# A trunk of S5, FoX and GLA layers on one core: f6 ahead of s40 in the MLPs, the first S5 layer's start in another order, and the final norm's means ahead of its turns

## The chip, the core and the metric

The program runs on one core of one Trainium2 chip. The metric is the time of one execution in microseconds (us), the median over runs. The engines are PE (matrix products; PEld are its weight loads), DVE (vector), ACT (scalar functions and copies), POOL (general) and SP, which here only issues DMAs. Each engine works through its own queue in order. DMA queue q1 holds the transfers that SP and ACT issue, q0 those that POOL issues.

## The reference

The input is one sequence of 256 positions with 1024 features, in f32. Four layers follow; each adds a mixer, an MLP and a per-layer embedding (PLE) to the residual h. The mixers are S5, FoX, GLA and S5 again.

```
for l in range(4):
    h += mixer_l(rmsnorm(h))                       # s5, fox, gla, s5
    h += relu(rmsnorm(h) @ w1)**2 @ w2             # MLP, 1024 -> 4096 -> 1024
    h += (p[l] @ W_pp) * sigmoid(rmsnorm(h) @ W_pg)
out = rmsnorm(h)

def s5_mixer(xn, ...):                             # 64 groups, 64 complex states each
    u = xn @ w_in
    dt = exp(log_dt); mag = exp(lr * dt)
    ab = mag * (cos(li * dt) + 1j * sin(li * dt))  # the decay of each state
    bbar = (ab - 1) / lambda * b                   # what B becomes
    x = u times bbar, per group
    s = scan over positions: s[t] = ab * s[t-1] + x[t]
    y = real(s times c) + d_skip * u
    z1, z2 = split(gelu(y) @ w_glu)
    return (z1 * sigmoid(z2)) @ w_out
```

rmsnorm divides by the root of the mean square of the 1024 features, so it needs the sum of squares over all of them before anything can be scaled; the kernel multiplies the unscaled products by that root afterwards.

## The kernel before

The residual h stays in the chip's memory with features on the partitions: eight tiles `H[k]` of 128 features by 256 positions, in pairs `HH[k]`. The program is written in a tile framework: the code names tiles and the framework puts the instructions in an order of its own for each engine, by its model of when operands are ready, and gives each tile a buffer. Three things hold that order: `in_order(...)` keeps the named engines in the order of the code, `keep_in_program_order` pins one DMA, and `issue_after(x)` puts what stands under it behind instruction x.

**Weights.** A weight unit is 256 rows by 512 columns. SP loads it as `raw`; ACT makes `whi`, the value rounded to a shorter format (L182), and DVE makes `wlo`, the rest (L184). A product takes three matmuls: whi times both halves of x, and wlo times the upper one. There are three `raw` and four `whi` and `wlo` buffers, so casts run a few units ahead.

**The MLP** works in blocks. `f`c computes hidden block c of 512 (four units of w1, four banks of accumulation): ACT copies a bank to `relu` (L247), DVE adds the other part (L248), squares the positive part (L386), and it is split into `s`. `s`c`r` multiplies block c by two units of w2 into output half r; the sums of four blocks are closed with `y` (also L247, L248). The string `MLP` sets the order of the blocks. Banks come by tag: f0 to f3, f6 and f7 use three banks `wk` and the bank `mk`, f4 and f5 use three `acc` and `mk`. The second products of the first output half use three `acc` and `po`, those of the second half, blocks 0 to 3, three `wk` and `po`, and s41 to s71 two `wk`. So f6, f7 and s01 to s31 share the `wk` banks, and s40 to s70 use others. Each step after the first also calls `further()`, which adds one step of the preparation of the last S5 layer, between the units.

**The first S5 layer's start** is in `s5_start`, branch `if first`. All 32 column pieces of `w_in` are products w0 to w7 of f32 weights without a split (eighths of 512 rows by 256 columns, `raw`, `wh`, `wl` and so on in turn are only their buffers). Step by step:

- PE warms up with 14 products of ones; ACT scales x from h and squares it (`sq`); PE adds the squares up over the features (`mean`, L1287).
- `s5_scalars` makes on DVE the decay's powers (`powers`, `cpow`, `F1`, `F8`), the table `ct` and, on POOL's queue, four DMAs that write it out as `tab` (L845), which is read back spread over partitions as `coef`.
- `z(0)`: the root. DVE makes `rrow` (L340), POOL raises it to the power −1/2 (L344). `z(1)`: DVE makes `diag` (L353) from it, and PE spreads that over partitions (L354), giving `rstd`.
- `f(0)`: `s5_spread`, 32 small products on PE (L855) that spread the table for the first quarter, so that the first quarter needs no `coef`.
- `bT` (L868, 512 KB a quarter) and `bc` (L879, 256 KB a quarter) are B and C. The steps named in `FIRST` then run quarter by quarter: `u` (L1165) scales w's product, `i` makes `wh` and `wl` out of bT and the table (L889 to L891), `r` makes `rot` (L911 to L914), `o` makes `qo` from bc (L929 to L933), `x` multiplies u by wh and wl on PE (L999), `y` makes the outputs (L1045).

Before the change bT of the quarters 0 and 1 and bc of quarter 0 are issued ahead of all of this.

**The final norm** (`final`) squares each H[k] on ACT, sums it over the features on PE against a column of 1/1024 (L1339), and turns H[k] to positions on partitions while it multiplies by the gain (L1333). When the last mean is there, DVE, POOL, then DVE and ACT scale the turned tiles by the root and SP writes them out.

Of the kernel before, what the change touches and what calls it, by code (L numbers as in the profile page):

```python
# [12 lines left out]
AF = mybir.ActivationFunctionType  # L13
ALU = mybir.AluOpType
# [20 lines left out]
WARM = 14  # L35


MLP = "f0 f1 f2 s00 f3 s10 s20 s30 s01 s11 f4 s21 f5 s31 s40 f6 f7 s50 s60 s70 s41 s51 s61 s71"


def _turn():
# [22 lines left out]
class Trunk:  # L64
# [783 lines left out]
    def s5_spread(self, b):  # L848

        out = []  # L850
        for i in range(2):
            ps = self.psum()
            for p in range(8):
                for g in range(2):
                    self.nc.tensor.matmul(ps[g * 64:(g + 1) * 64, p * 64:(p + 1) * 64], self.pick[:, p], self.ct[:, i, g, :], start=True, stop=True, skip_group_check=True)  # L855
            out.append(ps)
        return out

# [254 lines left out]
    def s5_start(self, l):  # L1113
# [3 lines left out]
        j = l // 3  # L1117
# [24 lines left out]
            units["h", i] = self.parts(units["h", i])  # L1142

        def w(i, between=None):
            b, i = i // 2, i % 2
            if i == 0:
                us[b] = self.psum((128, 2, T), "acc")
            ps = us[b]
            if first:
                raw = halves[2 * b + i]  # L1150
            else:
                hi, lo = units.pop(("h", 2 * b + i))
            for n in range(2):
                c = slice(n * 128, (n + 1) * 128)
                for k in range(4):
                    if first:
                        nc.tensor.matmul(ps[:, n], raw[:, k, c], x[4 * i + k], start=i == k == n == 0, stop=i == 1 and k == 3, skip_group_check=True)
                    else:
                        self.col(ps[:, n], v["x"][2 * i + k // 2][:, k % 2], hi[:, k, c], lo[:, k, c], i == k == n == 0, i == 1 and k == 3)
                if n == 0 and between:  # L1160
                    between()
# [30 lines left out]
        def j_(b):  # L1192
            bcs[b] = self.s5_fetch_out(j, b, self.tc.keep_in_program_order)
# [73 lines left out]
        if first:  # L1267
            halves = [self.raw0] + [self.half(w_in, i) for i in range(1, 8)]
            x = [self.t4("x", (128, 4, T), tag="x4") for _ in range(2)]
            x = [x[k // 4][:, k % 4] for k in range(8)]  # L1270
            bTs = {0: self.s5_fetch_in(j, 0)}
            j_(0)
            bTs[1] = self.s5_fetch_in(j, 1, self.tc.keep_in_program_order)
            scalars, v["ms"] = self.s5_scalars(j), self.psum((128, 2))

            def scaled(k):

                for i in range(2 * k, 2 * k + 2):
                    nc.scalar.activation(x[i], self.H[i], AF.Identity, scale=self.gains[:, l, i:i + 1])
                sq = self.f2("sq")  # L1280
                nc.scalar.activation(sq, self.HH[k], AF.Square)
                return sq
# [7 lines left out]
            with self.in_order(mybir.EngineType.Activation, mybir.EngineType.PE):  # L1290
# [12 lines left out]
                def between():  # L1303
                    next(scalars)

                    next(scalars)
                    sq.append(scaled(3))

                w(0, between)
# [4 lines left out]
                q.update(drain(scalars))  # L1314
                z(1)
                f(0)
            run("f1 j1")
        return lambda: run(FIRST if first else LATER)

    def final(self, out):  # L1320
# [11 lines left out]
            for half, t in enumerate(halves):  # L1332
                nc.tensor.matmul(hT[k // 4][half][:, k % 4], self.H[k][:, t], gain[:, k], start=True, stop=True)  # L1333

        for k in range(8):
            s = sq[k // 4][:, k % 4]
            nc.scalar.activation(s, self.H[k], AF.Square)
            for half, t in enumerate(halves):
                last = nc.tensor.matmul(ms[:, half:half + 1], s[:, t], self.mean, start=k == half == 0, stop=k == 7, skip_group_check=True)  # L1339
            if k < 6:  # L1340
                turn(k)
        with self.tc.issue_after(last.ins):
            turn(6)
            turn(7)
        r = self.inverse_root(ms)
        for half in range(2):
            o = self.t4("fin", (128, 2, 512))
# [69 lines left out]
```

## Time and profile before

| what | value |
|---|---|
| runs of the kernel | 1466.31, 1454.51, 1462.09 us |
| median | 1462.09 us |
| the profiled execution: its own time | 1458.21 us |
| its span in the profile | 1456.2 us |
| mean granted clock of PE | 0.987 |
| DMA in the span | 254.54 MB, mean 175 GB/s |
| ACT's and POOL's busy time | 717.2 us (49%), 100.9 us (7%) |

The span is the time from the first to the last record of the profiled execution, some 2 us shorter than its time. A row of the timeline gives start and length in us, the engine, the line of the code, the operation, what it writes and reads, how many records are joined in it (an f32 matmul leaves two), and in brackets the idle time of the engine before it with what ended that. A row of the waits gives the total of the waits in us, their number and the longest. A row of the stretches gives from:to, the length, for PE, PEld, DVE, ACT and POOL the busy time and the number of instructions, then PE's granted clock, the DMA share and GB/s. In the chain of work that ended last PE holds 63% of the span and every other engine 2% or less.

### The profile page before, as it was taken

What the parts mean: (1) busy time and instruction counts of PE and PEld (TensorE: products, weight loads), DVE (VectorE), ACT (ScalarE), POOL (GpSimd) and SP (SyncE); (2) the same over time, 40 slices, a digit from 0 to 9 for tenths busy, and PEclk for the clock granted to TensorE, in tenths of its full rate; (3) what the DMA queues carried; (4) which work ended last, traced back from release to release, by engine and by line L of the source; (5) the groups of instructions that cost most, each with busy time, mean ns of one, the idle gap of its engine ahead of it and who ended that gap; (6) DMA issues with size and microseconds to landing.
All of it is one profiled execution on the core that took longest, in us unless ns stands there. A gap on an engine that the chain in (4) does not pass through costs nothing.

```text
span 1456.2 us, 26681 instructions
## 1 busy us (share of the span) xinstructions
PE 1401.7 (96%) x10810; PEld 1264.3 (87%) x10810; DVE 1046.4 (72%) x1651; ACT 717.2 (49%) x1118; POOL 100.9 (7%) x167
## 2 busy tenths in 40 slices
PE   8999999999999999999999999999997899999997
PEld 7799988888998888889989598888996799888897
DVE  8995678775866678887667478786676946766764
ACT  3234564444654655445567355454562345545443
POOL 2000000010010000000004000000003100000020
PEclk9999999999999999999999999999998899999998
DMA  7534555557554456766655356565656545556561
GB/s 255 160 108 121 183 180 188 177 172 222 173 159 133 125 165 189 253 220 186 203 162 161 100 153 197 188 228 166 215 161 202 173 150 179 180 179 201 174 190 58
DMA packets 143227, 254.54 MB, mean 175 GB/s; under 512 B 21648, under 2 KB 32240, under 8 KB 143104
## 3 DMA queue, kind: packets, MB, share of 16 engines
q1 hardware_dynamic: 129856, 227.66, 50.4%
q0 software_dynamic: 7360, 23.73, 4.9%
q10 hardware_dynamic: 5888, 1.44, 0.4%
q8 instruction: 84, 1.38, 0.4%
q14 instruction: 39, 0.32, 0.1%
HBM read 242.15 MB, written 7.86 MB: 172 GB/s over the span
## 4 chain that ended last, share of the span: by engine, by line
PE 63%; DMA 2%; DVE 2%; ACT 2%; issue 0%; DVEq 0%; POOLq 0%; ACTq 0%; SPq 0%
PE wk L237 8%; PE acc L237 7%; PE wk L239 4%; PE wk L201 4%; PE wk L202 4%; PE wk L203 4%; PE acc L201 4%; PE acc L202 3%; PE acc L203 3%; PE acc L239 3%; PE mk L237 3%; PE po L237 2%; PE acc L262 1%; PE acc L261 1%; PE acc L263 1%; PE mk L239 1%
## 5 line engine op out<-in xcount | busy, mean ns | idle before, releaser
L184 DVE TENSOR_TENSOR wlo<-raw,whi 128x1024 fp32r<-128x1024 f32 x404 | 491.6, 1226 | 288.1 <-ACT whi L182 280.7
L182 ACT CAST whi<-raw 128x1024 fp32r<-128x1024 f32 x404 | 420.0, 1049 | 505.2 <-DMA raw<-mlp_w 85.4
L237 PE MATMUL wk<-x,whi 128*128 128x512 f32 x576 | 182.1, 401 | 7.8 <-DVE relu L248 7.8
L239 PEld LDWEIGHTS wk<-x,wlo 128*128 128x128 f32 x576 | 106.9, 191 | 22.9
L237 PE MATMUL acc<-s,whi 128*128 128x512 f32 x384 | 118.4, 397 | 2.7 <-ACT whi L182 2.7
L239 PE MATMUL wk<-x,wlo 128*128 128x256 f32 x576 | 113.3, 281 | 0.0
L237 PEld LDWEIGHTS wk<-x,whi 128*128 128x128 f32 x576 | 92.2, 191 | 11.9 <-DVE relu L248 8.9
L201 PE MATMUL acc<-x,whi 128*128 128x256 f32 x352 | 99.8, 287 | 1.8 <-DVE u L1165 1.0
L203 PE MATMUL acc<-x,wlo 128*128 128x256 f32 x352 | 99.9, 286 | 0.8 <-DVE wlo L184 0.8
L202 PE MATMUL acc<-x,whi 128*128 128x256 f32 x352 | 99.4, 285 | 0.0
L239 PEld LDWEIGHTS acc<-s,wlo 128*128 128x128 f32 x384 | 70.4, 190 | 15.8 <-DVE wlo L184 0.5
L237 PE MATMUL mk<-x,whi 128*128 128x512 f32 x256 | 81.4, 395 | 0.0
L239 PE MATMUL acc<-s,wlo 128*128 128x256 f32 x384 | 74.8, 283 | 0.0
L202 PE MATMUL wk<-s,whi 128*128 128x256 f32 x256 | 72.4, 283 | 0.0
L201 PE MATMUL wk<-s,whi 128*128 128x256 f32 x256 | 72.4, 283 | 0.0
L203 PE MATMUL wk<-s,wlo 128*128 128x256 f32 x256 | 72.3, 283 | 0.0
L201 PEld LDWEIGHTS acc<-x,whi 128*128 128x128 f32 x352 | 66.9, 191 | 3.3 <-issue 1.8
L203 PEld LDWEIGHTS acc<-x,wlo 128*128 128x128 f32 x352 | 67.3, 191 | 1.6 <-DVE wlo L184 1.3
L202 PEld LDWEIGHTS acc<-x,whi 128*128 128x128 f32 x352 | 67.2, 192 | 0.2
L237 PEld LDWEIGHTS acc<-s,whi 128*128 128x128 f32 x384 | 60.0, 189 | 4.5 <-ACT whi L182 2.9
L237 PE MATMUL po<-s,whi 128*128 128x512 f32 x192 | 60.5, 397 | 0.0
L237 PE MATMUL wk<-s,whi 128*128 128x512 f32 x192 | 59.1, 395 | 0.0
(402 smaller groups left out, 3358.3 us busy)
## 6 DMA issues: line engine op xcount, KB each, us to landing
raw<-mlp_w SPq DMA_DIRECT2D x256, 512.0 KB, 4.3
raw<-s_w_glu SPq DMA_DIRECT2D x32, 512.0 KB, 4.2
raw<-ple_gate SPq DMA_DIRECT2D x32, 512.0 KB, 3.5
raw<-fox_w_in SPq DMA_DIRECT2D x24, 512.0 KB, 3.7
raw<-gla_w_in SPq DMA_DIRECT2D x24, 512.0 KB, 3.9
raw<-s_w_out SPq DMA_DIRECT2D x16, 512.0 KB, 4.1
kept<-kept POOLq DMA_DIRECT2D x12, 512.0 KB, 5.2
raw<-s_w_in SPq DMA_DIRECT2D x11, 512.0 KB, 4.9
```

The costliest lines, as they stand in the source:

```text
L182: nc.scalar.copy(hi, raw)
L184: self.last_lo = nc.vector.tensor_tensor(lo, raw, hi.bitcast(F32), ALU.subtract)
L201: mm(ps, hi, x[:, 0], start=first, stop=False, skip_group_check=True)
L202: mm(ps, hi, x[:, 1], start=False, stop=False, skip_group_check=True)
L203: self.last_mm = mm(ps, lo, x[:, 0], start=False, stop=last, skip_group_check=True)
L237: mm(ps[n], hi[:, i, s], v[i], start=first and i == 0, stop=False, skip_group_check=True)
L239: self.last_mm = mm(ps[n][:, 0], lo[:, i, s], v[i][:, 0], start=False, stop=last and i == UK - 1, skip_group_check=True)
L261: mm(ps[half], a[:, 0, t], hi[:, k], start=k0 + k == 0, stop=False)
L262: mm(ps[half], a[:, 0, t], lo[:, k], start=False, stop=False)
L263: mm(ps[half], a[:, 1, t], hi[:, k], start=False, stop=k0 + k == nk - 1)
```

## The change

Three parts. In the MLPs f6 comes ahead of s40 rather than behind it. In the first S5 layer the DMAs of bT 0, bc 0 and bT 1 are issued on POOL's queue behind those that write the table, and the products w2 to w7 are kept behind the last product of `s5_spread`. In the final norm the squares of the first four H are added in pairs on DVE, so that 12 products sum the means rather than 16, and the means stand ahead of the turns of their group.

```diff
-MLP = "f0 f1 f2 s00 f3 s10 s20 s30 s01 s11 f4 s21 f5 s31 s40 f6 f7 s50 s60 s70 s41 s51 s61 s71"
+MLP = "f0 f1 f2 s00 f3 s10 s20 s30 s01 s11 f4 s21 f5 s31 f6 s40 f7 s50 s60 s70 s41 s51 s61 s71"
...
-                    self.nc.tensor.matmul(ps[g * 64:(g + 1) * 64, p * 64:(p + 1) * 64], self.pick[:, p], self.ct[:, i, g, :], start=True, stop=True, skip_group_check=True)
+                    self.last_mm = self.nc.tensor.matmul(ps[g * 64:(g + 1) * 64, p * 64:(p + 1) * 64], self.pick[:, p], self.ct[:, i, g, :], start=True, stop=True, skip_group_check=True)
...
         def w(i, between=None):
+            with self.tc.issue_after(v["mm"].ins) if "mm" in v else nullcontext():
+                product(i, between)
+
+        def product(i, between):
             b, i = i // 2, i % 2
...
-            bTs = {0: self.s5_fetch_in(j, 0)}
-            j_(0)
-            bTs[1] = self.s5_fetch_in(j, 1, self.tc.keep_in_program_order)
             scalars, v["ms"] = self.s5_scalars(j), self.psum((128, 2))
...
                     next(scalars)
+                    bTs[0] = self.s5_fetch_in(j, 0, self.tc.keep_in_program_order)
+                    j_(0)
+                    bTs[1] = self.s5_fetch_in(j, 1, self.tc.keep_in_program_order)
                     sq.append(scaled(3))
...
                 f(0)
+                v["mm"] = self.last_mm
             run("f1 j1")
...
-        for k in range(8):
-            s = sq[k // 4][:, k % 4]
-            nc.scalar.activation(s, self.H[k], AF.Square)
+        def mean(x, first, last):
             for half, t in enumerate(halves):
-                last = nc.tensor.matmul(ms[:, half:half + 1], s[:, t], self.mean, start=k == half == 0, stop=k == 7, skip_group_check=True)
-            if k < 6:
+                self.last_mm = nc.tensor.matmul(ms[:, half:half + 1], x[:, t], self.mean, start=first and half == 0, stop=last, skip_group_check=True)
+
+        for k in range(4):
+            nc.scalar.activation(sq[0][:, k], self.H[k], AF.Square)
+        nc.vector.tensor_tensor(sq[0][:, 0:2], sq[0][:, 0:2], sq[0][:, 2:4], ALU.add)
+        with self.tc.issue_after(self.last_mm.ins):
+            for k in range(2):
+                mean(sq[0][:, k], k == 0, False)
+            for k in range(4):
                 turn(k)
-        with self.tc.issue_after(last.ins):
-            turn(6)
-            turn(7)
+        for k in range(4, 8):
+            nc.scalar.activation(sq[1][:, k - 4], self.H[k], AF.Square)
+        for k in range(4, 8, 2):
+            with self.tc.issue_after(self.last_mm.ins):
+                for i in range(2):
+                    mean(sq[1][:, k + i - 4], False, k + i == 7)
+            with self.tc.issue_after(self.last_mm.ins):
+                for i in range(2):
+                    turn(k + i)
```

On PE in the first layer's MLP, before, where s31 ends (`po_2964`), s40 starts (`acc_3435`, from block 4's `s_3073`); x is the scaled input of the MLP, the numbers tell tiles apart:

```order
L239 MATMUL po_2964<-s_2648,wlo_3390 128x256 x2
L237 MATMUL acc_3435<-s_3073,whi_3441 128x512 x2
L239 MATMUL acc_3435<-s_3073,wlo_3442 128x256 x2
L237 MATMUL acc_3436<-s_3073,whi_3441 128x512 x2
L239 MATMUL acc_3436<-s_3073,wlo_3442 128x256 x2
```

and, still before, where f6 ends and f7 starts:

```order
L237 MATMUL mk_3488<-x_2197,whi_3557 128x512 x2
L239 MATMUL mk_3488<-x_2197,wlo_3558 128x256 x2
L237 MATMUL wk_3613<-x_2194,whi_3619 128x512 x2
L239 MATMUL wk_3613<-x_2194,wlo_3620 128x256 x2
L237 MATMUL wk_3613<-x_2195,whi_3641 128x512 x2
```

On PE after the change f6 follows s31, with three units in `mk` ahead of the first `wk`:

```order
L239 MATMUL po_2964<-s_2648,wlo_3390 128x256 x2
L237 MATMUL mk_3440<-x_2194,whi_3443 128x512 x2
L239 MATMUL mk_3440<-x_2194,wlo_3444 128x256 x2
L237 MATMUL mk_3440<-x_2195,whi_3465 128x512 x2
L239 MATMUL mk_3440<-x_2195,wlo_3466 128x256 x2
L237 MATMUL mk_3440<-x_2196,whi_3487 128x512 x2
L239 MATMUL mk_3440<-x_2196,wlo_3488 128x256 x2
L237 MATMUL wk_3437<-x_2194,whi_3443 128x512 x2
```

and f7 follows s40:

```order
L239 MATMUL acc_3547<-s_3074,wlo_3574 128x256 x2
L237 MATMUL po_3548<-s_3074,whi_3573 128x512 x2
L239 MATMUL po_3548<-s_3074,wlo_3574 128x256 x2
L237 MATMUL wk_3613<-x_2194,whi_3619 128x512 x2
L239 MATMUL wk_3613<-x_2194,wlo_3620 128x256 x2
```

What moved: s40, whose banks nobody near it uses, now stands between the two blocks that share `wk`, and f6 stands right behind s31, which shares `wk` with it too.

On PE at the start of the first S5 layer the pieces of w are those lines with `acc`; `diag,ones` is the root's product, `ct,pick` the spread, `U,wh` the first x. Both orders in one piece, from the first means' end on:

```order
-L1157 MATMUL acc<-x,wl 128x256 x7
-L1287 MATMUL wk<-mean,sq 128x1 x4
-L1157 MATMUL acc<-x,wh 128x256 x8
-L1157 MATMUL acc<-x,wl 128x256
-L1157 MATMUL acc<-x,raw 128x256 x5
+L1288 MATMUL wk<-mean,sq 128x1 x4
+L1161 MATMUL acc<-x,wh 128x256 x8
 L354 MATMUL wk<-diag,ones 128x256
 L855 MATMUL wk<-ct,pick 64x64 x32
```

What moved: half of w2 and w3 stood ahead of the root's product before; now only w1 does, and w2 and w3 (`wl` and `raw`) come behind the spread.

On DVE the same place, before: `F8` and `F` are powers, `rrow` the root's row, `diag` what PE waits for, `dd` and `rot` the steps behind:

```order
L353 TENSOR_SCALAR diag_364<-ident_86,rrow_275 128x128 x2
L706 TENSOR_TENSOR F8_305<-F8_305,prod_215 128x32x2
L704 TENSOR_TENSOR F8_305<-F8_305 128x32x3
L705 TENSOR_TENSOR prod_215<-F8_305 128x96
L704 TENSOR_TENSOR F8_305<-F8_305 128x32x3
L705 TENSOR_TENSOR prod_215<-F8_305 128x96
L706 TENSOR_TENSOR F8_305<-F8_305,prod_215 128x32x3 x2
L825 TENSOR_TENSOR dd_358<-eye16_102,sd_152 32x512
L911 TENSOR_TENSOR rot_442<-F1_304,F8_305 128x1024
```

and after:

```order
L706 TENSOR_TENSOR F8_305<-F8_305,prod_209 128x32x3 x2
L825 TENSOR_TENSOR dd_358<-eye16_102,sd_146 32x512
L911 TENSOR_TENSOR rot_442<-F1_304,F8_305 128x1024
L911 TENSOR_TENSOR scratch_443<-F1_304,F8_305 128x1024
L911 TENSOR_TENSOR rot_700<-F1_304,F8_305 128x1024
L353 TENSOR_SCALAR diag_364<-ident_86,rrow_275 128x128 x2
```

What moved: diag stood ahead of the last powers, dd and the L911 products, and stands behind three of them now.

## The prediction

> **What bounds the kernel now.** I read the page's first lines, then PE's waits, then the timeline around each wait that the change touches, and the granted clock by stretches.
>
> ```profile
> span 1456.2 us, 26681 instructions
> PE 1401.7 (96%) x10810; PEld 1264.3 (87%) x10810; DVE 1046.4 (72%) x1651; ACT 717.2 (49%) x1118; POOL 100.9 (7%) x167
> PE wk L237 <- DVE relu L248: 7.8, 6, 2.5
> ```
>
> PE is busy for 1401.7 of 1456.2 us, so the change, which leaves PE's work nearly as it was, can win at most some of the 54.5 us in which PE stands still, and what PE loses at a lower clock. The third line is the largest entry among PE's waits. Four of its six waits are the places where f7 follows f6, one in each layer's MLP:
>
> ```profile
> 311.86 0.73 PE L237 MATMUL wk<-x,whi 128*128 128x512 f32 x2 [1.17 <-DVE relu L248]
> 652.62 0.73 PE L237 MATMUL wk<-x,whi 128*128 128x512 f32 x2 [2.49 <-DVE relu L248]
> 1000.56 0.74 PE L237 MATMUL wk<-x,whi 128*128 128x512 f32 x2 [1.89 <-DVE relu L248]
> 1365.20 0.74 PE L237 MATMUL wk<-x,whi 128*128 128x512 f32 x2 [1.04 <-DVE relu L248]
> ```
>
> f7 writes the three `wk` banks that f6 has just filled and that ACT and DVE must empty first: 1.17 + 2.49 + 1.89 + 1.04 = 6.59 us. Two of these gaps cost more than their length. In the stretches the column after the five engines is the granted clock:
>
> ```profile
> 653.23:656.64 3.41, 3.41 (x13) 2.93 (x12) 3.33 (x6) 1.24 (x2) 0.00 (x0) 0.50 0.64 174
> 1001.38:1004.80 3.42, 3.42 (x13) 2.85 (x12) 3.05 (x5) 0.95 (x2) 0.00 (x0) 0.50 0.66 196
> 335.79:339.20 3.41, 3.41 (x12) 2.72 (x11) 3.22 (x4) 1.58 (x2) 0.00 (x0) 0.50 0.45 144
> 653.57 1.05 PE L237 MATMUL wk<-x,whi 128*128 128x512 f32 x2
> 654.85 1.05 PE L237 MATMUL wk<-x,whi 128*128 128x512 f32 x2
> 633.17 0.63 PE L237 MATMUL acc<-s,whi 128*128 128x512 f32 x2
> 633.87 0.85 PE L237 MATMUL acc<-s,whi 128*128 128x512 f32 x3
> ```
>
> After the gaps of 2.49 and 1.89 us PE worked one stretch of 3.41 us at clock 0.50. There a group of four (two 512-wide, two 256-wide) takes 654.85 − 653.57 = 1.28 us; at full clock 633.87 − 633.17 = 0.70. One stretch therefore costs 3.41 × (1 − 0.70/1.28) = 1.55 us. The stretches start whole multiples of 3.413 us apart (1001.38 − 653.23 = 102 × 3.413), so the same gap can halve the clock or not, as it falls on that grid. The gaps of 1.17 and 1.04 us halved nothing.
>
> **MLP: f6 before s40.** No instruction is added or removed. With s40 between f6 and f7, f7's `wk` banks have eight groups of 0.70 = 5.6 us in which to be emptied; the worst gap needed 2.5 us. So 6.59 us of waits and 2 × 1.55 = 3.1 us of half clock go. What is late next is the new seam, where f6 now follows s31 and writes banks from which y is still being read. The order starts f6 with its first three or four units in the `mk` bank, 2.1 to 2.6 us of work ahead of `wk`. The seam of the second MLP is the tightest:
>
> ```profile
> 634.09 1.21 DVE L184 TENSOR_TENSOR wlo<-raw,whi 128x1024 fp32r<-128x1024 f32 x1
> 635.23 1.07 DVE L248 TENSOR_TENSOR y<-wk,y 128x256 f32<-128x256 f32 x3
> ```
>
> s31 ends at 633.17. The first of three y additions ends about 635.64, 2.5 us later: just covered. The third unit's wlo is ready at 635.30, 2.1 us after the seam, and the new order wants it after two groups and a half, 1.86 us: 0.3 us of wait. The other layers are earlier or ask less; I take 0.4 us for all four. Bounds: nothing new (gain 9.7), or one gap like the old ones at each seam (a gain of 3.1 to 5). MLP: 6.6 + 3.1 − 0.4 = **9.3 us**. PE's single 2.70 us wait in s70 of the first MLP and its half-clock stretch (the row at 335.79 above) aren't touched, but their place on the grid moves, so 1.6 us may come or go.
>
> **First S5 layer.**
>
> ```profile
> 0.00:11.87 11.87, 7.13 (x44) 6.77 (x45) 9.59 (x67) 7.25 (x15) 4.37 (x21) 0.99 0.78 254
> bT<-s_bT POOLq DMA_DIRECT2D x2, 512.0 KB, 6.8
> bc<-s_bc POOLq DMA_DIRECT2D x1, 256.0 KB, 7.1
> 11.87 3.49 PE L1157 MATMUL acc<-x,raw 128*128 128x256 f32 x8 [2.85 <-DMA raw<-s_w_in]
> 15.77 1.89 PE L1157 MATMUL acc<-x,raw 128*128 128x256 f32 x8
> 17.50 0.95 PE L1287 MATMUL wk<-mean,sq 128*128 128x1 f32 x8
> 16.64 2.13 POOL L845 DMA_DIRECT2D tab<-ct  x4 [11.62 <-ACT ct L840]
> ```
>
> Up to 11.87 us the DMA moved 11.87 × 254 = 3.0 MB, and 1.28 MB of that is the two bT and the bc that the change moves behind the table. At that rate w_in's first half comes several us sooner, so I take the whole 2.85 us wait as gone (bounds 0 and 2.85) and w0 at 9.0. w0's first eight pieces also took 15.29 − 11.87 = 3.42 us where the next eight took 17.50 − 15.77 = 1.73 (15.29 is where the first run ends), half clock again: 1.7 us. Together 4.55 us.
>
> What it adds is a wait. w2 and later products now stand behind the spread, the spread behind the diagonal product, and that waits for DVE:
>
> ```profile
> 12.93 1.48 DVE L929 TENSOR_TENSOR qo<-bc,cpow 128x1280 f32<-128x1280 f32 x1
> 22.81 0.16 DVE L340 TENSOR_SCALAR rrow<-wk 128x2 f32<-128x2 f32 x1 [4.88 <-PE wk L1287]
> 23.97 0.47 DVE L353 TENSOR_SCALAR diag<-ident,rrow 128x128 f32<-128x128 f32 x2
> 25.54 0.67 DVE L825 TENSOR_TENSOR dd<-eye,sd 32x512 f32<-32x512 f32 x1
> 26.14 1.21 DVE L911 TENSOR_TENSOR rot<-F,F 128x1024 f32<-128x1024 f32 x1
> 29.55 0.67 DVE L913 TENSOR_TENSOR rot<-rot,scratch 128x512 f32<-128x512 f32 x1
> 28.76 0.59 PE L354 MATMUL wk<-diag,ones 128*128 128x256 f32 x2
> 31.30 1.56 PE L1157 MATMUL acc<-x,raw 128*128 128x256 f32 x6
> 32.70 3.62 PE L1157 MATMUL acc<-x,wh 128*128 128x256 f32 x16
> ```
>
> In the new order DVE makes diag after the powers of F, dd and three L911 products. dd began at 25.54; without the idle 4.88, the L929 at 12.93 (1.40 to the next start) and diag itself (0.39), which now come elsewhere, that is 18.87; dd takes 26.14 − 25.54 = 0.60 and the three L911 29.55 − 26.14 = 3.41. So diag begins at 22.9 and PE gets it at 23.1. The root isn't what is late: the last means now stand ahead of w1 and end by 15, and POOL's power, behind three more DMA issues (four took 2.13 us, so 1.6), is there by about 16. PE has from 9.0 on w0 and w1 (32 pieces, 4 × 1.73 = 6.9), two means (at most 0.95 each) and the table's 0.5 us between 15.29 and 15.77: free at about 18.4. It then stands for 4.7 us, more than any gap so far, and about 1.0 us is lost at half clock after it (0 to 1.7 by the grid). Diag product and spread take 31.30 − 28.76 = 2.5, w2 and w3 another 32 pieces, 6.9: 23.1 + 2.5 + 1.0 + 6.9 = 33.5 us, against 32.70 before. x0 now stands right behind w3 and needs wl, which DVE ends at about 34.6: from 23.3 it has L913 and L914 (0.6 each), three L929 (1.40 each), and u, two wh and two pairs of small ones, by their starts before 0.9, 2.3, 1.5 and 1.2, 11.3 us in all. With the way to PE, 34.7: PE is 34.7 − 32.7 = 2.0 us later there. bT and bc, issued at 12 to 16 and first read at 24.5, have some 9 us against the 6.8 and 7.1 us that they took.
>
> Against that DVE, which worked on after 22.81 with the idle 4.88 us behind it, is now ahead by about that much, and these waits of PE on it or on what it feeds should go:
>
> ```profile
> 54.93 0.33 PE L999 MATMUL wk<-U,wh 64*64 64x64 f32 x4 [0.52 <-DMA U<-u]
> 58.88 2.08 PE L1045 MATMUL mk<-qo,P 64*64 64x64 f32 x64 [1.64 <-DVE P L1024]
> 70.51 0.39 PE L202 MATMUL acc<-g,whi 128*128 128x256 f32 x1 [0.46 <-DVE g L1229]
> 74.33 0.39 PE L201 MATMUL acc<-g,whi 128*128 128x256 f32 x1 [2.25 <-DVE u L1165]
> ```
>
> 0.52 + 1.64 + 0.46 + 2.25 = 4.9 us in all. Net 4.9 − 2.0 = **2.9 us**; bounds −2.0 (none of these waits goes) and 4.9 (the later start at x0 is made up).
>
> **The final norm.**
>
> ```profile
> 1445.08 0.95 PE L1339 MATMUL wk<-mean,sq 128*128 128x1 f32 x8
> 1445.89 0.47 PE L1333 MATMUL mk<-gain,h 128*128 128x128 f32 x2
> 1447.19 0.16 DVE L340 TENSOR_SCALAR rrow<-wk 128x2 f32<-128x2 f32 x1 [3.25 <-PE wk L1339]
> 1439.60 0.76 DVE L471 TENSOR_TENSOR z<-wk,rstd 128x256 f32<-128x256 f32 x2 [4.80 <-PE wk L203]
> ```
>
> Four of 16 mean products go; eight records, 1445.89 − 1445.08 = 0.81 us of PE's path. The DVE addition that replaces them lies where DVE has time (its idle 4.80 us); PE runs without a gap there, and the last means still come last but for four turns, so the root and the end move by as much: **0.8 us**. It is at least 0 (if the last turns bind instead) and hardly more, since nothing else of the chain is touched.
>
> **Sum.** 9.3 + 2.9 + 0.8 = 13.0 us. The profiled execution took 1458.2, which makes 1445.2. It lies 3.9 below the median of the runs, 1462.09; the mean of these four executions is 1460.3. I go from there: **1447 us**, 1.0% below the median.
>
> **Rivals.** (1) The S5 layer gives nothing or loses: DVE's stall of 4.7 us is sure by the order, while the later waits go only if DVE keeps its lead. Its bound of −2.0 makes 1452. (2) The seam takes over part of the MLP's wait: the y additions and the casts share DVE, and one old-size gap in two layers, 2 × 2.5, makes 1452. (3) The other side: every f6 starves at its seam. Four units' casts, at 1.21 us of DVE each, are asked for in 2.6 us. From 1.9 us, with the half clock 3.45 per layer, four seams eat the 13.4 us that the rest brings; at 2.5 each they cost 4 × 4.05 = 16.2 and the time is 1463. Against it: three or four units' buffers are filled ahead in the row shown. (4) The clock is not at stake: the Trainium skill, "TensorE: Matmul & The Clock Gate", section "Why this matters for your kernels", asks only for no idle gaps beyond about 3 us, one idle window costing the full rate. By that rule, taken strictly, gaps of 1.9 to 2.9 us cost only themselves. As a mechanism of this kernel it would take back 3.1 + 1.7 us and leave the 1.0 us after the new stall: 1452. The rows at 0.50 after 1.89 and 2.49 us speak against it. (5) More than summed: no wait at x0 and the untouched 2.70 us gap losing its half clock, 1447 − 0.9 − 1.6 − 2 (S5 towards its upper bound) = 1442.
>
> **Numbers.** Forecast 0.42, (1) 0.20, (2) 0.14, (3) 0.05, (4) 0.04, (5) 0.15. The runs of before alone spread from 1454.5 to 1466.3, so each case has some 4 us to either side; 1439 to 1457 leaves out the far side of (5) and most of (3). One per cent, about what a measurement of this kernel can tell, is 1447.5 below and 1476.7 above: half of the forecast, (5) and a little of (1) and (2) make 0.41 for faster; 0.03 of (3) with a seam beyond 3 us for slower; the rest 0.56.
>
> **What would show it.** MLP: no wait on relu at f7, clock 1.0 there, and waits under 0.5 us at f6's start. S5: w0 at about 9, PE idle from 18.4 to 23.1 on DVE's diag, x0 at 34.7, and no wait of 2.25 before the second output. Tail: rrow 0.8 us closer after the last gate product. It is wrong if waits above 1 us stand at f6, if w0 still waits for its weights, or if S5's later waits stay.

## The result and the profile after

| | before | changed |
|---|---|---|
| median of nine runs | 1458.16 us | 1446.62 us |
| lowest and highest | 1454.51, 1466.31 | 1443.82, 1450.58 |
| span of the profiled execution | 1456.2 us | 1444.8 us |

The ratio is 0.9924 with a 95% interval of [0.9906, 0.9942]: the changed kernel is 0.8% faster, within the 1% that was called hard to tell. 1446.62 us stands beside a forecast of 1447. The sum behind that number is another matter: its terms were 9.3, 2.9 and 0.8 us, and one of them has the wrong sign. First the page and two of PE's waits in the changed kernel's profile:

```profile
span 1444.8 us, 26675 instructions
PE 1398.2 (97%) x10802; PEld 1261.9 (87%) x10802; DVE 1047.9 (73%) x1652; ACT 719.8 (50%) x1118; POOL 99.8 (7%) x167
PE wk L354 <- DVE diag L353: 5.0, 1, 5.0
PE wk L237 <- DVE relu L248: 1.1, 2, 0.8
```

The waits on relu fell from 7.8 to 1.1 us (two waits at the end of f0, which the change leaves alone); a new one of 5.0 us, for diag, is the largest that the change brings. To see where the time went, the start of the same product is compared in both traces. The mean products of line 333 are the marks: one run of them stands at the start of each MLP and one behind its end, here the first MLP's in the kernel before and in the changed one.

```profile
203.09 1.05 PE L333 MATMUL wk<-mean,sq 128*128 128x1 f32 x8 [0.72 <-DVE relu L248]
```

```profile
205.33 1.05 PE L333 MATMUL wk<-mean,sq 128*128 128x1 f32 x8 [0.75 <-DVE relu L248]
```

The first S5 layer ends 205.33 − 203.09 = 2.24 us later. All marks in this way, as differences to the profiled execution of the kernel before, stage by stage in us (minus is time won; the other kernels are told below, and each row is a single execution):

| kernel | first S5 | MLP 1 | MLP 2 | MLP 3 | MLP 4 | last means to end of turns | all other stages |
|---|---|---|---|---|---|---|---|
| the change | +2.24 | −6.15 | −4.25 | −3.26 | −1.32 | −0.89 | +2.24 |
| MLP's order alone | +1.22 | −6.14 | −3.45 | −3.21 | −1.31 | 0 | +0.12 |
| S5 start alone | +2.12 | −2.97 | −0.30 | −1.62 | +0.47 | 0 | +0.91 |
| MLP and final norm | −0.06 | −6.15 | −4.34 | −3.37 | −1.34 | −0.89 | +1.18 |
| diag first | +2.59 | −6.15 | −4.34 | −2.85 | −1.32 | −0.88 | −0.59 |
| no hold | +0.56 | −6.15 | −3.30 | −3.30 | −1.33 | −0.89 | +0.85 |
| hold only | +5.14 | −6.14 | −3.58 | −3.15 | −1.33 | −0.89 | +2.37 |
| four qo | +9.06 | −6.15 | −3.92 | −3.52 | −1.33 | −0.89 | +2.80 |
| diag first, four qo | +5.43 | −6.14 | −4.00 | −3.09 | −1.33 | −0.89 | −1.43 |
| buffers without the hold | +4.90 | −6.14 | −4.29 | −3.13 | −1.32 | −0.89 | +5.31 |
| the table later | +0.38 | −6.14 | −3.89 | −2.43 | −1.33 | −0.89 | +3.86 |
| PE kept busy | +1.73 | −6.15 | −4.25 | −3.08 | −1.31 | −0.89 | −2.65 |

So the MLPs gave 15.0 us, the final norm 0.9, the S5 start took 2.2, and layers that the change doesn't touch took 2.2 more. One of these, in the timeline and the stretches of the changed kernel:

```profile
505.31 0.66 PE L551 MATMUL po<-pT,v 128*64 128x128 f32 x8 [1.11 <-ACT pT L544]
506.65 0.50 PE L201 MATMUL acc<-o,whi 128*128 128x256 f32 x2 [0.68 <-ACT o L277]
504.15:507.56 3.41, 1.62 (x14) 1.13 (x14) 1.92 (x2) 1.69 (x3) 0.00 (x0) 1.00 0.54 165
507.56:510.97 3.41, 3.41 (x17) 3.41 (x18) 0.69 (x1) 0.25 (x1) 0.00 (x0) 0.50 0.41 147
```

The two waits of 1.11 and 0.68 us have the same length before the change, where no half clock follows them. Here they fall into one stretch of 3.41 us of the clock's grid, which leaves PE 1.62 us of work in it, and the next stretch is at half clock.

Where f7 now begins in the first MLP, and the largest wait at the new seam of all four, in the changed kernel:

```profile
312.49 0.40 PE L239 MATMUL po<-s,wlo 128*128 128x256 f32 x2
312.73 0.63 PE L237 MATMUL wk<-x,whi 128*128 128x512 f32 x2
```

```profile
977.87 0.73 PE L237 MATMUL mk<-x,whi 128*128 128x512 f32 x2 [0.24 <-ACT whi L182]
```

f7 follows s40 without a gap; f6's seam costs 0.24 us in one layer and nothing above 0.15 in the others.

The S5 start of the changed kernel on PE, then on DVE, then the clock (the granted clock is the third column from the end):

```profile
8.85 3.43 PE L1161 MATMUL acc<-x,raw 128*128 128x256 f32 x8
25.35 1.22 PE L354 MATMUL wk<-diag,ones 128*128 128x256 f32 x2 [4.98 <-DVE diag L353]
37.05 0.33 PE L999 MATMUL wk<-U,wh 64*64 64x64 f32 x4
73.64 0.39 PE L201 MATMUL acc<-g,whi 128*128 128x256 f32 x1 [1.17 <-DVE u L1169]
82.39 0.27 PE L999 MATMUL wk<-U,wh 64*64 64x64 f32 x3 [0.85 <-issue]
95.38 0.38 PE L201 MATMUL acc<-g,whi 128*128 128x256 f32 x1 [1.70 <-DVE W L1026]
```

```profile
16.84 0.16 DVE L340 TENSOR_SCALAR rrow<-wk 128x2 f32<-128x2 f32 x1 [1.95 <-PE wk L1288]
24.83 0.47 DVE L353 TENSOR_SCALAR diag<-ident,rrow 128x128 f32<-128x128 f32 x2
61.87 1.49 DVE L929 TENSOR_TENSOR qo<-bc,cpow 128x1280 f32<-128x1280 f32 x1 [4.93 <-PE mk L1045]
```

```profile
5.80:9.21 3.41, 3.06 (x27) 2.95 (x27) 2.75 (x25) 3.41 (x9) 0.00 (x0) 1.00 1.06 354
9.21:12.62 3.41, 3.41 (x10) 2.09 (x9) 3.38 (x33) 0.97 (x3) 0.00 (x0) 0.50 1.09 385
19.45:22.86 3.41, 0.92 (x5) 0.46 (x3) 3.41 (x13) 0.00 (x0) 1.36 (x3) 1.00 1.02 408
22.86:26.27 3.41, 0.92 (x2) 0.50 (x2) 3.41 (x6) 1.28 (x4) 0.81 (x2) 0.50 1.02 299
22.86:29.69 6.83, 4.34 (x62) 3.69 (x64) 6.83 (x9) 1.65 (x5) 0.81 (x2) 0.50 0.70 213
```

w0 begins at 8.85 as forecast, but at half clock again; the stall for diag is there (4.98 us), and two stretches at half clock stand at its end, 22.86 to 29.69: its 4.98 us leave 0.92 us of work in each of two stretches of the grid, and each is followed by one at half clock. The first x begins at 37.05, where the prediction put it at 34.7. And DVE, which was to be ahead, stands 4.93 us until 61.87 for a buffer that PE still reads.

### The profile page after: what moved, and what is told of

Its sections match the earlier page's. It is cut to its first block, busy times and chain, and to the rows that moved or that the text cites. A ratio compares the mean times of both kernels' runs of the same rounds, so it can differ in the third digit from the quotient of the medians.

```text
span 1444.8 us, 26675 instructions
## 1 busy us (share of the span) xinstructions
PE 1398.2 (97%) x10802; PEld 1261.9 (87%) x10802; DVE 1047.9 (73%) x1652; ACT 719.8 (50%) x1118; POOL 99.8 (7%) x167
## 4 chain that ended last, share of the span: by engine, by line
PE 62%; DVE 2%; DMA 2%; ACT 2%; issue 1%; DVEq 0%; POOLq 0%; ACTq 0%; SPq 0%
PE wk L237 9%; PE acc L237 7%; PE wk L239 4%; PE wk L201 4%; PE wk L202 4%; PE wk L203 4%; PE acc L201 3%; PE acc L239 3%; PE acc L202 3%; PE acc L203 3%; PE mk L237 3%; PE po L237 2%; PE mk L239 1%; PE acc L262 1%; PE acc L261 1%; PE acc L263 1%
```

## The experiments

The first four ask which part gives what, and whether the stall for diag is what costs in S5. All kernels use the lines of the diff shown above; a short diff says what each has of it.

**The MLP's order alone.** Against the kernel before:

```diff
-MLP = "... f5 s31 s40 f6 f7 s50 ..."
+MLP = "... f5 s31 f6 s40 f7 s50 ..."
```

> Only the MLP's order of blocks is changed; S5 and the final norm are as before. Theory A (the order itself takes away the wait on relu at f7 in all four layers, and also PE's 2.70 us wait in s70 of the first MLP, since the table's DMAs then meet the weight loads at another point): the four MLPs give 6.1 + 4.3 + 3.3 + 1.3 = 15.0 us, as between the two traces; span about 1441 us, ratio about 0.990. Rival B (the 2.70 us wait and its half-clock stretch went only because the new S5 start shifted what follows): that wait is still in the trace and the gain is 9 to 11 us, ratio about 0.993.

Measured: ratio 0.9907 [0.9882, 0.9931], span 1443.4 us. Theory A holds in its main point: the first MLP gives 6.14 us though the S5 start is the old one, and PE's 2.70 us wait in it is gone. Rival B falls. (The prediction and the expectations put that wait in s70; counted in units behind f7, it stands ahead of the second unit of s60.) The four MLPs give 14.1 us of the expected 15.0. Why the wait went, the table's place or something else, this run was not made to tell; its trace helps with that under "The table later".

**The S5 start alone.** The change's hunks in `s5_spread` and `s5_start`, with the old MLP string and the old final norm.

> Only the first S5 layer's start is changed. Theory A (it loses, as the two traces say: the first MLP starts 2.2 us later): span about 1458.5 us, ratio about 1.0015, with PE waiting some 5 us for diag and two stretches at clock 0.50 behind it. Rival B (it gains and the 2.2 us are an accident of the one profiled execution, or the gain in the first MLP belongs to it): span at or below 1454 us, ratio 0.998 or less.

Measured: ratio 1.0019 [1.0004, 1.0034], slower, though by little. The first MLP starts 2.12 us later, nearly the 2.24 of the full change. The span, 1454.8 us, lies under the expected 1458.5: the profiled execution is the fastest of this kernel's twelve (1456.49 to 1463.10 us), and two MLPs were shorter in it with the old order of blocks. In the first, as B had right in part, the wait behind f7 shrank:

```profile
338.55 0.73 PE L237 MATMUL acc<-s,whi 128*128 128x512 f32 x2 [0.49 <-ACT whi L182]
```

In the third, the wait on relu stayed, but the stretch behind it kept its clock, as the timeline and then the stretches show; that is most of the 1.62 us in the table, near the 1.55 that the prediction put on one stretch:

```profile
1000.52 0.74 PE L237 MATMUL wk<-x,whi 128*128 128x512 f32 x2 [1.84 <-DVE relu L248]
998.77:1002.18 3.41, 1.66 (x9) 1.47 (x10) 3.27 (x6) 2.56 (x7) 0.00 (x0) 1.00 0.60 166
1002.18:1005.60 3.42, 3.42 (x21) 2.94 (x20) 2.73 (x5) 0.83 (x2) 0.00 (x0) 1.00 0.72 257
```

So the 2.70 us wait depends on how loads happen to meet; the new order removes it in every run that has it, and a shift of 2 us can shrink it too.

**MLP and final norm, S5 as before.**

```diff
+MLP = "... f5 s31 f6 s40 f7 s50 ..."
...
+        def mean(x, first, last):
```

> The MLP's order and the final norm are changed, the first S5 layer is as before. Theory A: 15.0 + 0.9 us less than before, span about 1440.3 us, ratio about 0.989, that is 2 us better than the full change. Rival B (the S5 start pays for itself): ratio at or above that of the full change, 0.9924.

Measured: ratio 0.9906 [0.9881, 0.9931], span 1441.3 us, 3.5 below the full change's. The medians point the way of A (the full change has 0.9924), but their intervals overlap; it is the run before this one that shows S5's loss by itself.

**Diag first on DVE.**

```diff
-                q.update(drain(scalars))
-                z(1)
+                for _ in range(7):
+                    next(scalars)
+                z(1)
+                with self.tc.issue_after(self.diag.ins):
+                    q.update(drain(scalars))
...
+            with self.tc.issue_after(v["diag"].ins) if "diag" in v else nullcontext():
+                rots[b] = drain(self.s5_rot(q, b)), decay(b)
```

> The full change, but DVE makes diag ahead of the last powers of F8, dd and the L911 products, which are held behind it. Theory A (the 5.0 us wait for diag is DVE's order, and it alone halves the clock behind it): the wait is about 0 to 1 us, no stretch at clock 0.50 stands at 23 to 30 us, the first x is 4 to 6 us earlier, and the whole is 4 to 6 us shorter than the full change: span about 1439 us, ratio about 0.988. Rival B (DVE is co-bound in this layer, so that what is moved behind diag is late for the outputs of the first three quarters): the wait for diag goes but later waits on P, W and u grow by as much, and the first MLP starts no more than 2 us earlier than in the full change: ratio 0.991 to 0.9925.

Measured: ratio 0.9934 [0.9911, 0.9958]. PE's timeline shows that the wait for diag is gone; these are the first x and the waits that come in its place:

```profile
18.90 0.70 PE L354 MATMUL wk<-diag,ones 128*128 128x256 f32 x2
29.48 0.33 PE L999 MATMUL wk<-U,wh 64*64 64x64 f32 x4 [0.76 <-DMA U<-u]
...
53.69 2.92 PE L1045 MATMUL mk<-qo,P 64*64 64x64 f32 x64 [3.17 <-DVE P L1024]
71.00 0.39 PE L201 MATMUL acc<-g,whi 128*128 128x256 f32 x1 [1.16 <-DVE u L1169]
79.22 0.33 PE L999 MATMUL wk<-U,wh 64*64 64x64 f32 x4 [0.32 <-issue]
...
93.93 0.38 PE L201 MATMUL acc<-g,whi 128*128 128x256 f32 x1 [3.65 <-DVE W L1026]
```

The root's product comes 25.35 − 18.90 = 6.45 us earlier than in the change, and the first x 37.05 − 29.48 = 7.6 us, as no half clock stands between them. From there on PE waits 3.17 + 1.16 + 0.32 + 3.65 = 8.3 us, against 1.17 + 0.85 + 1.70 = 3.7 in the change, and the stretch behind the first of these waits (54.64 to 58.05) is at half clock. At the last output of the S5 layer, at 127 us, 1.1 us of that are left, and a stretch at half clock that follows it (from 129.73, after two waits of 0.70 and 0.67 us that every run has) takes them too: the first MLP starts 0.35 us later. Rival B holds in this trace: nearly all that PE wins before 30 us goes later, on waits for DVE and on the half clock behind one of them.

The next runs ask why it can't be kept: buffers, the hold, or the moved loads.

**Four qo buffers**, in the full change and with diag first:

```diff
-"qo": 2, "tm": 3, "s2": 10,
+"qo": 4, "tm": 3, "s2": 5,
```

> The full change with four buffers for qo rather than two (and five rather than ten of the small s2 tiles, to make room). In the full change DVE stands for 4.93 us at 61.9 us because the third quarter's qo needs the buffer that PE's first output still reads, and PE later waits for DVE in the third quarter (1.17 + 0.85 + 1.70 us). Theory C (the S5 start cannot gain because DVE's lead cannot be stored past the second quarter: both of its qo buffers are held until PE's first output is done): the 4.93 us idle is gone, PE's three waits shrink by 2.5 to 3.7 us, and the first MLP starts 2.5 to 3.7 us earlier than in the full change, whole ratio about 0.990. Rival D (PE is the bound up to 65 us and what DVE lacks behind is made up of work that can't be done ahead, the scans and what follows x): the idle time only moves, and the first MLP starts no more than 1 us earlier.

> As the run with diag first on DVE, with four qo buffers. There the wait for diag and its half-clock stretches were gone, yet PE waited 3.17 + 1.16 + 0.32 + 3.65 us later and the first MLP started only 1.1 us earlier than in the full change. Theory C: with the qo buffers free the late waits shrink by 4 us or more, and the first MLP starts 2.5 to 4 us earlier than in the kernel before, ratio about 0.987. Rival D: the waits stay and the start is within 1 us of that run's.

Measured: 0.9951 [0.9931, 0.9970] and 0.9910 [0.9887, 0.9933]. The first MLP starts 9.06 and 5.43 us later than in the kernel before, so S5 is 6.8 and 2.8 us worse than without the buffers. Theory C fell, and D's "within 1 us" too, since it came out later. In the second, three stretches at half clock stand from 54.07 to 64.31 where the run without the buffers has one; at some 1.5 us each, an estimate from the stretches told above, they can be all of its 2.8 us. And the edit halves the number of small s2 tiles too, which no run does alone. The first run did not test C cleanly, as another wait took the place on DVE:

```profile
45.83 1.49 DVE L929 TENSOR_TENSOR qo<-bc,cpow 128x1280 f32<-128x1280 f32 x1 [2.53 <-DMA bc<-s_bc]
66.43 1.49 DVE L929 TENSOR_TENSOR qo<-bc,cpow 128x1280 f32<-128x1280 f32 x1 [3.97 <-DMA bc<-s_bc]
```

**No hold**: the rule is taken out, the loads stay moved.

```diff
-                v["mm"] = self.last_mm
```

> The full change without the rule that keeps w2 to w7 behind the spread; the DMAs of bT and bc stay behind the table. Theory A (the 5 us wait for diag exists because PE has nothing else in its queue there): PE has w2, w3 and a part of w4 ahead of diag, the wait is about 0 and no stretch at clock 0.50 stands behind it; the loads' early landing stays. What the rule was to give, an earlier spread, is lost. I expect the first MLP 1 to 3 us earlier than in the full change, ratio about 0.991. Rival B (DVE sets the end of this layer whatever PE does first): the first MLP starts within 0.7 us of the full change.

Measured: ratio 0.9905 [0.9880, 0.9930]. w0 to w3 and part of w4 stand ahead of the root's product, PE has no wait up to 35 us, and the first MLP starts at +0.56, 1.68 us earlier than in the full change. Theory A is borne out: the wait for diag and the half clock behind it are gone, and the 1.68 us are somewhat more than executions of one start differ by (1.2 us, below). Later waits come in this run too, the longest 3.78 us at 55.68.

**Hold only**: the loads are back at the start, the rule stays.

```diff
+            bTs = {0: self.s5_fetch_in(j, 0)}
+            j_(0)
+            bTs[1] = self.s5_fetch_in(j, 1, self.tc.keep_in_program_order)
             scalars, v["ms"] = self.s5_scalars(j), self.psum((128, 2))
```

> The full change with bT and bc issued at the start as before, while w2 to w7 stay behind the spread. Theory A (moving the loads gives the earlier first weights, about 3 us, whose use the half clock then halves): w0 waits for its weights again until 11 to 12 us, as before, and DVE, which has bc early, makes diag ahead of the L911 products, so that the wait for diag is under 3 us. The first MLP starts 0 to 3 us later than in the kernel before, ratio about 0.992. Rival E (the loads' move is what costs, by bT and bc that come late for the first x): the first MLP starts earlier than in the kernel before.

Measured: ratio 0.9939 [0.9923, 0.9956]. The first MLP starts at +5.14 us, later than both theories expected; E falls, and of A the direction holds (PE had no wait for diag at all), not the size. With the runs that share the old S5 start the two edits make a square of starts of the first MLP:

| | loads as before | loads behind the table |
|---|---|---|
| no hold | 0, −0.06, +0.38, +1.22 (four kernels) | +0.56 |
| hold | +5.14 | +2.24, +2.12 (two kernels) |

The four values in one field are the same program up to there, so an entry is good to about 1 us. By these executions the hold costs 1.6 us with the loads moved and some 4 us without; the move of the loads by itself gives nothing that shows, and helps only where the hold is. How much of the 4 us is the order itself stays open: the run with the hold only has four stretches at half clock ahead of the first MLP, the four kernels beside it one to three.

**Buffers without the hold**, with a third bc buffer:

```diff
-"qo": 2, "tm": 3, "s2": 10, "a2": 4, "wt": 4, "g2": 2,
+"qo": 4, "tm": 3, "s2": 4, "a2": 4, "wt": 4, "g2": 3,
```

> The kernel without the hold (w2 to w7 free, loads behind the table, MLP and final norm as in the change), with four buffers for qo and three for bc (four small s2 tiles rather than ten make room). In the run with four qo alone DVE's idle time only changed its cause, from the qo buffer to the load of bc (2.53 + 3.97 us). Theory C (DVE's lead is lost for want of buffers): with bc's third buffer both waits shrink below 1.5 us in sum, PE's waits in the third and fourth quarter shrink, and the first MLP starts 1.5 to 4 us earlier than without the extra buffers, ratio about 0.988. Rival D (what DVE does ahead isn't what PE later waits for): the first MLP's start differs from that of the run without the hold by under 1 us, or is later, ratio 0.990 or more.

Measured: ratio 0.9946 [0.9927, 0.9965]; the first MLP starts at +4.90. From 40 to 80 us neither the qo buffer nor bc makes DVE wait now, yet it stands as long, for PE's second x:

```profile
65.60 1.23 DVE L1009 TENSOR_TENSOR W<-wk,rot 128x1024 f32<-128x1024 f32 x1 [5.22 <-PE wk L999]
```

Rival D holds by the start of the first MLP. The reading of it, that the pause at 60 us is PE's and DVE's turn-taking (DVE's scan for one quarter, PE's output, PE's next x) and that a free buffer only changes the name of what DVE waits for, fits this trace and was not tried by itself. Why S5 became some 4 us longer with the buffers isn't settled: PE's order changed with them, and the small s2 tiles fell from ten to four.

**The table later.** The kernel with MLP and final norm, and

```diff
-            if i and i < 16:
+            if i and i < 17 and i != 14:
```

> The MLP's order and the final norm as changed, S5 as before, but each step of the preparation for the last S5 layer from the fourteenth on comes one block later, so that the table's DMAs in the first MLP come at the end of f7. Theory A (the 2.70 us wait in s70 of the first MLP went because the table's DMAs no longer meet the loads of s50 to s70): ACT's longest wait for raw there grows to 6 us or more and PE waits 0.5 to 3 us in the first MLP again. Rival F (it went because f6 ahead of s40 has more weights ready, whatever the table does): no PE wait over 0.3 us in the first MLP's second half.

Measured: ratio 0.9895 [0.9867, 0.9923]; the first MLP gives its 6.14 us, and PE has no wait there. ACT's waits for loads in that MLP up to 346 us, first before the change, then in this run:

```profile
ACT whi L182 <- DMA raw<-mlp_w: 13.3, 4, 8.5
```

```profile
ACT whi L182 <- DMA raw<-mlp_w: 2.0, 2, 1.1
```

This alone does not decide for F, since the table came later than was meant. PE waited for the second unit of s60. In this run its load is issued at 316.02 and takes 3.7 us, while the table is written from 329.74 and read back from 334.60, behind all loads of s50 to s70. The load that does meet the reads there, at 338.85, takes 9.0 us; ACT waits 6.24 us for it, and PE does not:

```profile
334.60 0.52 POOL L874 DMA_DIRECT2D coef<-tab  x1 [2.71 <-DMA tab<-ct]
346.86 1.05 ACT L182 CAST whi<-raw 128x1024 fp32r<-128x1024 f32 x1 [6.24 <-DMA raw<-mlp_w]
```

What decides is the same load in the kernel before and in the run of the MLP's order alone. SP issues it at 323.95 and at 319.98, and s50 begins on PE at 323.69 and 323.44. From the issue to the landing it took, first before, then in that run:

```profile
raw<-mlp_w SPq DMA_DIRECT2D x1, 512.0 KB, 9.8
```

```profile
raw<-mlp_w SPq DMA_DIRECT2D x1, 512.0 KB, 8.1
```

In both it met the reads of the table, which began at 322.63 and 319.02, and was slow. With the new order it went out 3.5 us ahead of s50 rather than 0.3 us behind it, and landed 4.6 us into s50 and s60 rather than 10.1; PE asks for the unit some 8.5 us in (it stopped at 334.93 − 2.70 = 332.23 before). So F holds: the new order sends the loads out earlier, and the slow one is in time, whether it meets the table or not.

**PE kept busy.**

```diff
                 w(1)
+                for _ in range(13):
+                    nc.tensor.matmul(warm, self.ones, self.ones, start=True, stop=True)
                 q.update(drain(scalars))
```

> The full change with 13 idle products of ones (26 records of 128 by 128, about 4.7 us by the warm-up's 28 in some 5.0 us) behind w1, where PE waits for diag; their result is not used. Theory A (the standstill of 5.0 us halves the clock for two stretches, 2.4 us): no stretch at clock 0.50 stands at 23 to 30 us, the spread and w2, w3 run at full clock, and the first x starts 2 to 2.5 us earlier; what of it reaches the first MLP is bounded by DVE, 0.5 to 2.4 us. Rival G (products of 128 columns don't count as work for the clock, or the half clock comes from the small products of the spread): the stretches at 0.50 stay.

Measured: ratio 0.9895 [0.9874, 0.9916], span 1439.6 us. The stretch that was at half clock, and the first x:

```profile
23.40:30.20 6.80, 6.50 (x84) 5.66 (x85) 6.80 (x9) 0.41 (x2) 0.00 (x0) 1.00 0.67 208
33.45 0.33 PE L999 MATMUL wk<-U,wh 64*64 64x64 f32 x4
```

Theory A holds: with these products in the gap the clock stays at 1.00 (no other kind of work was tried; PE still waits 2.07 us for diag), and the first x begins 37.05 − 33.45 = 3.6 us earlier. Of it, 1.65 us come because w0 met no half clock this time and diag came sooner; the other 1.95 us, from the root's product to the first x, are the clock. Of the 3.6 us the first MLP sees 2.24 − 1.73 = 0.5.

Six kernels (MLP alone, MLP and final norm, no hold, diag first with four qo, table late, PE kept busy) have ratios from 0.9895 to 0.9910, all under the change's 0.9924. Their intervals overlap with its own, so no one of them is shown to be faster than the change by its times; that the S5 start should be left as it was rests on the run of it alone, whose interval begins at 1.0004.

## Why the prediction was right, and where it was not

**The total** was right to half a microsecond, but by errors that cancel. The MLPs gave 5.7 us more than their term, S5 5.1 us less than its own, and untouched stages took 2.2. That makes 11.4 us between the two spans where 13.0 were forecast; the starting point made up for it, as 1460.3 us lies 2.1 above the profiled execution of the kernel before. So that it came out to half a microsecond is luck.

**MLP: the mechanism was right, the size too small.** f7's waits and both half-clock stretches went, and the seam cost 0.24 us where 0.4 was taken. The second, third and fourth MLP gave 4.25, 3.26 and 1.32 us, 8.8 against 8.2 by the terms (2.49 + 1.89 + 1.04 and two times 1.55, less 0.3 of the 0.4 for seams). With one order of blocks the second and third varied between kernels by about 1 us (−3.30 to −4.35 and −2.43 to −3.52), so the 0.6 us between them and the terms say little. The step that failed is the sentence that PE's 2.70 us wait in the first MLP and its stretch "aren't touched": that alone is 2.70 + 1.55 = 4.25 us of its 6.15. f6 and s40 change places, the loads that stood behind a full set of buffers go out 3.7 us earlier against s50, and ACT's wait for loads from 318 to 346 us falls from 13.3 to 8.2 us, its longest from 8.5 to 4.3, so that PE has its weights. An order diff shows which instruction stands where, not that the loads behind it start earlier.

**S5: the stall was forecast well and its consequence was not.** By the steps: w0 at 9.0 (measured 8.85), the stall 4.7 us (4.98), its cause DVE's diag behind the L911 products. Wrong were four steps. First, the 1.7 us of half clock in w0 did not go: the stretch from 9.21 is at 0.50 though PE was busy for 3.06 of the 3.41 us ahead of it; the wait of 2.85 us was not its only cause. It goes by the execution: the runs without the hold, with diag first and with PE kept busy have no half clock there. The wait itself does too: with the loads as before, the run of MLP and final norm began w0 at 10.04 after 0.98 us. Second, diag came at 24.83 rather than 22.9: of DVE's idle 4.88 us, taken as gone, 1.95 stayed, since rrow stands ahead of more powers in the new order and waits for the means. These were late by w0's half clock; in the run with PE kept busy the wait of rrow is 0.37 us. Third, 1.0 us lost at half clock was 2.2: half of the 4.34 us of work in the two stretches. Together the first x began at 37.05 for 34.7. The fourth is the one that decides: "DVE ... is now ahead by about that much", 4.9 us. It was, until 57 us; then it stood 4.93 us. The waits of 0.52, 1.64 and 0.46 us that the prediction let go did go, 2.25 became 1.17, and 0.85 and 1.70 us came in the third quarter. One reading of the orders was off as well: of w2 and w3 not half stood ahead of the root's product before, but 8 and 5 of 8 products each, which at the prediction's 6.9 us for both is an estimated 5.6 us of work that the hold takes away where PE now stands. The runs with diag first and with PE kept busy show what lies behind it: 6.45 and 3.6 us won at the start of this layer are 1.1 and 0.5 us at its end. The prediction's first rival, that S5 gives nothing or loses, with a bound of −2.0, is what happened, 0.2 us beyond the bound. (Rival 5 takes 0.9 us for the wait at x0, where the prediction's own 34.7 − 33.5 makes 1.2.)

**The Trainium skill's rule** ("TensorE: Matmul & The Clock Gate", section "Why this matters for your kernels") asks for no idle gaps beyond about 3 us. The rival built on it falls: waits of 1.11 and 0.68 us that shared one stretch with little else halved the next, and one of 3.65 us with diag first halved nothing (last section). The run with idle products, at 1.00 from 23.40 to 30.20 us, agrees with what the Trainium skill has behind the rule (same page, section "What's actually happening"), that the clock follows how busy PE has been.

**Final norm:** 0.89 us where 0.8 was forecast. The last mean and the root's row in the changed kernel:

```profile
1434.81 0.95 PE L1342 MATMUL wk<-mean,sq 128*128 128x1 f32 x8
1435.79 0.16 DVE L340 TENSOR_SCALAR rrow<-wk 128x2 f32<-128x2 f32 x1 [2.35 <-PE wk L1342]
```

Counted from the last product of line 333 (1426.64 before, 1416.14 here), rrow starts 20.55 us later in the kernel before and 19.65 us later here. PE has no wait on DVE's addition.

**The chances** were fair: 1446.62 is 0.8% under the other median, inside the 56% of "same", and the range of 1439 to 1457 holds it.

## What to carry to other kernels

A step that is late because two engines hand work to each other is not helped by starting one of them earlier: before a wait is counted as gone, follow the engine that is to be ahead to the next thing it waits for. Two blocks that share accumulators are worth parting wherever a block with others can stand between them; here the MLPs gave 15 us, more than the whole change won, though an estimated 4.25 of it came from loads that went out earlier. Two single profiled executions of this kernel differ by some us in stages that are the same, so a small change is read stage by stage, and a stage more than once.

## What the runs showed that was not expected

A stage that no edit touches, from the third MLP's end to the fourth's start (the last S5 layer), differed by −2.68 us (PE kept busy) to +1.51 us (MLP and final norm) from the kernel before; it has three stretches at half clock in the first, six in the second and five before. (In the runs with other buffers or the later table, whose edits do reach that stage, it was from 1.47 us shorter to 5.66 us longer.) The same goes for the first 203 us: four kernels with the same S5 start stood at 0, −0.06, +0.38 and +1.22 us, with one, two, two and three stretches at half clock. Both go with the granted clock: which stretch of 3.41 us falls to half clock depends on where short waits lie on a grid that does not start with the kernel (the first half-clock stretch starts at 11.52 before and at 9.21 after the change, which are not whole stretches apart). The wait of 2.25 us at 74.33 before the change halved nothing; in the run of the MLP's order alone the same wait, 2.24 us at 74.09, lay within one stretch and halved the next:

```profile
70.65:74.06 3.41, 1.20 (x11) 0.99 (x9) 3.41 (x7) 0.00 (x0) 0.00 (x0) 1.00 0.47 137
74.06:77.47 3.41, 3.38 (x22) 3.16 (x24) 3.38 (x5) 0.55 (x2) 0.00 (x0) 0.50 0.29 67
```

So what the traces point at is PE's work within a stretch of the grid, 1.20 and 1.62 of 3.41 us in the two cases shown, not the length of one wait. In the run with diag first even PE's wait of 3.65 us, which fell on two stretches, halved nothing, while later in the same run two short waits did:

```profile
88.77:92.19 3.42, 1.51 (x7) 0.97 (x6) 3.42 (x6) 0.00 (x0) 0.00 (x0) 1.00 0.01 1
92.19:95.60 3.41, 1.67 (x14) 1.68 (x15) 3.41 (x7) 0.00 (x0) 0.00 (x0) 1.00 0.06 14
126.32:129.73 3.41, 2.04 (x26) 1.47 (x21) 0.98 (x2) 2.17 (x3) 0.00 (x0) 1.00 0.00 0
129.73:133.14 3.41, 3.41 (x18) 3.41 (x18) 1.98 (x2) 0.89 (x2) 0.00 (x0) 0.50 0.35 104
```

Busy time is not the whole rule either: the stretch after 1.51 us of work kept its clock, that after 2.04 us did not, and in the run with PE kept busy 2.04 us from 125.86 halved nothing. And the clock can fall where PE is hardly idle: in the changed kernel the stretch from 5.80 had PE busy for 3.06 us, much of it with means whose moving side is one column wide, and the next one was at 0.50. Whether such products count as little work for the clock was not tried.
